# Splitting the weight operands of a Strassen-like matmul two at a time, in double-size tiles

## The chip, the cores and the metric

One core of one Trainium2 chip runs the kernel. Its engines are TensorE (PE: matmuls, and PEld for its weight loads), VectorE (DVE), ScalarE (ACT), GpSimd (POOL) and the queues that start transfers (SP above all). The metric is the device time of one execution in microseconds (us); the lower, the better. Each engine works off its own instructions in a fixed order, and one that waits holds up all behind it on that engine.

## The reference, cut to what matters

One layer of a decoder trunk over x (1024 tokens, 1024 channels) and 256 memory tokens. Nearly all of the work is matrix products with 1024 x 1024 weights:

```
h  = rms_norm(x, norm_g)
z  = h @ w_in                      # 11 blocks of 1024 columns
u  = gelu(z[U]);  v = layer_norm(gelu(z[V]))
br_a = u * (causal 128x128 mix of v inside each chunk, 8 groups, + b_s) * silu(z[GA])
glu  = z[BA] * sigmoid(z[BB])
br_b = silu(layer_norm(depthwise_causal_conv(glu, 31 taps))) * silu(z[GB])
br_c = cross_attention(z[Q], rms_norm(mem), w_kv) * silu(z[GC])
merged = sum over n of sigmoid(z[M0 + n]) * (br_n @ w_branch[n])
y = rms_norm(x + merged @ w_out, final_norm_g)
```

All of it is float32. To keep float32's accuracy on TensorE, an operand is split into a rounded high part and the remainder (hi and lo, both in the type fp32r), and a product is the sum of three: hi by hi, hi by lo, lo by hi.

## The kernel before

**Stages.** The kernel first makes keys and values of the memory and branch v. Then come 40 "pairs": in four rounds p = 0..3, ten blocks of w_in each (i = 0..9: BB, BA, U, GA, GC, GB, Q and three merge-gate blocks), and each pair computes two 128-channel rows of a block for all 1024 tokens. After the pairs come the projections of branches a and c with the attention between them, and then two more large products (branch b's projection and w_out), called the output stages here, and the final norm.

**A pair** (`pair`, L463 to L518) is a 2 x 2 block product with seven instead of eight block products. Its weights are two raw tiles r0 and r1 of 128 x 1024, loaded by SP; their halves are a11, a12 and a21, a22. DVE forms s1 = a21 + a22 (L460), s2 = s1 - a11 (L461), s3 = a11 - a21 (L479) and s4 = a12 - s2 (L480). Each of the seven weight operands a11, a12, s2, s1, s3, a22, s4 (128 x 512) is split by `operand`: ACT casts the high part (L74), DVE subtracts it (L75) to get the low part. `prod` (L448) then issues 12 matmuls of 128 x 512 per operand: for each of four k the high part twice, against the high and the low part of the other matrix, and after these the low part once. The seven products go to three PSUM banks x, z and y: x<-B (with a11) and z<-B (a12), x<-T (s2), y<-T (s1), x<-T (s3), and, put off into the next pair as fin1 and fin2, x<-T (a22) and y<-B (s4). ACT copies x out between (p1 at L466, u2 at L489, u3 at L498); DVE adds the halves of the result together in the tiles ca and cb (L476, L501, L511). In the trace the raw operands' tiles read `op<-raw`, the sums' `op<-sum`.

**What sets the order.** Tiles come from rings: `op` has 6 tiles of 128 x 2 x 512, `sum` 4 and `half` 4 of 128 x 512, `raw` 3 of 128 x 1024, `slot` 39 of 128 x 1024. A tile that is taken waits until the tile's last user is done. A scheduler orders the instructions of each engine when the program is built; no table in the kernel fixes them, beside a few that are kept in program order. Between the pair's steps, `fill` lets DVE do a few of the conv branch's 120 tap steps per round (L553: one multiply-add over 128 x 994 to 1023). The pair with the block GA ends with `ugate` (L624 to L636): DVE multiplies by u (L624), 32 small matmuls on PE mix v (L630), and DVE scales (L632) and multiplies four times (L636). Its instructions stand in the pair after the next on DVE, that is at i = 5. Each round also prepares sums of weight blocks in `wsums`: loads on SP, adding transfers on POOL, a split of 128 x 1024 (`wsh<-ws` on ACT, `ws<-ws,wsh` on DVE), and two stores to DRAM that POOL issues through L149 (`sw<-wsh` and `sw<-ws`). The tile `wsh` is of the `slot` ring, as ca and cb are.

**The output stages** take their operands through `gop` (a tile of the `op` ring each) and `gop2` (a `sum` and a `half` tile) in turn, and `oprod` (L979) issues their matmuls.

Of the kernel before, what the change touches and what calls it, by code (L numbers as in the profile page):

```python
# [16 lines left out]
P = 128  # L17
# [4 lines left out]
H = 512  # L22
# [17 lines left out]
def trunk(ctx, tc, xt, x, memt, wf, wv, wkf, wkv, mem, wbr, wb1, wo, wst, bs, cols, fng, out):  # L40
# [13 lines left out]
    def nm(s):  # L54
        uid[0] += 1
        return f"{s}_{uid[0]}"

    def slot(dt=F32, shape=(P, 1024), s="s"):
        return slots.tile(list(shape), dt, tag="slot", name=nm(s))

    def op(shape=(P, 2, H), s="op"):
        return wpool.tile(list(shape), F32R, tag="op", name=nm(s), bufs=NOP)

    def half(s="u"):
        return wpool.tile([P, H], F32, tag="half", name=nm(s), bufs=NHALF)

    def bank(s="b"):
        return bank1.tile([P, H], F32, tag="b", name=nm(s))
# [4 lines left out]
    def split(src, hi, lo):  # L73
        A.copy(hi, src)  # L74
        V.tensor_tensor(lo, src, f(hi), ALU.subtract)  # L75
# [9 lines left out]
        return raw  # L85

    def wchunk(src, raw=None):
        hi, lo = op((P, 1024), "whi"), op((P, 1024), "wlo")
        split(raw_load(src) if raw is None else raw, hi, lo)
        return hi, lo  # L90

    def flat(ps):
        return ps.rearrange("p a b -> p (a b)")
# [165 lines left out]
    for g in range(2):  # L259
        pst = [bank() for _ in range(4)]  # L260
        for j in range(4):
            i = 4 * g + j
            if i == 0:
                hi, lo = op((P, 1024), "whi"), op((P, 1024), "wlo")
                for kk2 in range(2):
                    v = slice(kk2 * H, (kk2 + 1) * H)
                    ksplit(kraw[0][:, v], hi[:, v], lo[:, v])
                    mem_gain(kk2)
            elif g:
                hi, lo = wchunk(None, kraw[i])  # L270
            else:
                hi, lo = op((P, 1024), "whi"), op((P, 1024), "wlo")
                ksplit(kraw[i], hi, lo)
                if g == 0:
                    mem_gain(2 * j)
                    mem_gain(2 * j + 1)
            for kk2 in range(2):
                k = 2 * j + kk2
                for e in range(4):
                    ks = slice(kk2 * H + e * P, kk2 * H + (e + 1) * P)  # L280
                    for n, (w, m) in enumerate(((hi, mhi), (hi, mlo), (lo, mhi))):
                        T.matmul(pst[e][:, :M], w[:, ks], m[k], start=(k == 0 and n == 0),
                                 stop=(k == KT - 1 and n == 2))
            kload(i + 3)
            if i < MT:
                sload(mtok[i], mem[i * P:(i + 1) * P, :])
            elif i < 5:
                x_load(2 * i - 4)
                x_load(2 * i - 3)
            else:  # L290
                v_load(i - 5)
                x_load(i + 1)
            if i == 3:
                for t in range(MT):
                    square(mtok[t], mss[:, t:t + 1])
                mr = mean_rsqrt(mss, MT, RMS_EPS)
                mdg = diagonals(mr, MT)
            if i == 5:
                spread(mdg, mrb, bank)
            if i >= 4:  # L300
                x_gain(i - 4)
            if i >= 6:
                for _ in range(2):
                    k_out(*late.pop(0))
        if g == 0:
            k3 = half("k3")
            A.copy(k3[:, :M], pst[3][:, :M])
            pst[3] = k3
        late.extend((4 * g + e, pst[e]) for e in range(4))
# [134 lines left out]
    def prod(ps, w, m, start, stop):  # L444
        for k in range(4):
            ks = slice(k * P, (k + 1) * P)
            for j, (a, b) in enumerate(((0, 0), (0, 1), (1, 0))):
                T.matmul(ps, w[:, a, ks], m[k][:, b, :], start=(start and k == 0 and j == 0),  # L448
                         stop=(stop and k == 3 and j == 2), skip_group_check=not start)

    def operand(src):
        o = op()
        split(src, o[:, 0, :], o[:, 1, :])
        return o

    def pair(blk, p, consume, fill=lambda: None, last=False):
        r0, r1 = raw_load(wf[blk, 2 * p]), raw_load(wf[blk, 2 * p + 1])
        a11, a12, a21, a22 = r0[:, :H], r0[:, H:], r1[:, :H], r1[:, H:]
        s1, s2, s3, s4 = [wpool.tile([P, H], F32, tag="sum", name=nm("sum"), bufs=NSUM) for _ in range(4)]
        V.tensor_tensor(s1, a21, a22, ALU.add)  # L460
        V.tensor_tensor(s2, s1, a11, ALU.subtract)  # L461
        o11 = operand(a11)
        x, z = bank("x"), bank("z")  # L463
        prod(x, o11, B[0][0], True, True)
        p1 = half("p1")
        A.copy(p1, x)  # L466
        fill()
        if pend:
            pend.pop(0)()
        fill()  # L470
        ca, cb = slot(s="ca"), slot(s="cb")

        def second():
            o12 = operand(a12)
            prod(z, o12, B[1][0], True, True)
            V.tensor_tensor(ca[:, :H], z, p1, ALU.add)  # L476
            fill()

        V.tensor_tensor(s3, a11, a21, ALU.subtract)  # L479
        V.tensor_tensor(s4, a12, s2, ALU.subtract)  # L480
        if not last:
            second()
        if pend:
            pend.pop(0)()
        fill()
        os2 = operand(s2)
        prod(x, os2, T2, False, True)
        u2 = half("u2")
        A.copy(u2, x)  # L489
        fill()  # L490
        os1 = operand(s1)
        y = bank("y")
        prod(y, os1, T1, True, True)
        fill()
        os3 = operand(s3)
        prod(x, os3, T3, False, True)
        u3 = half("u3")
        A.copy(u3, x)  # L498
        if last:
            second()  # L500
        V.tensor_tensor(cb[:, H:], y, u3, ALU.add)  # L501
        fill()
        o22 = operand(a22)
        os4 = operand(s4)

        def fin1():
            prod(x, o22, T4, False, True)

        def fin2():
            prod(y, os4, B[1][1], False, True)  # L510
            V.tensor_tensor(ca[:, H:], y, u2, ALU.add)  # L511
            consume(ca, cb, x)

        pend.extend((fin1, fin2))
# [286 lines left out]
    def att_q(n):  # L801
        hd, tb = divmod(n, 2)
        if hd not in kv:
            kv_load(hd)
        qh, ql = slot(F32R, (P, 2, H), "qh"), slot(F32R, (P, 2, H), "ql")
        for d in range(2):
            qf = wpool.tile([P, H], F32, tag="sum", name=nm("qf"), bufs=NSUM)
            nc.sync.dma_start(out=qf, in_=qdram[2 * hd + d][:, tb * H:(tb + 1) * H])
            split(qf, qh[:, d, :], ql[:, d, :])
        unit[n] = (qh, ql)  # L810
# [132 lines left out]
    def swload(w, i, tag):  # L943
        r = []
        for j in range(2):
            hl = [op((P, 1024), "sw") if tag else slot(F32R, s="sw") for _ in range(2)]
            b = (SUMB, SUMO)[w][i]
            if i == "1" or len(b) > 1:
                for v in range(2):
# [15 lines left out]
            split(v, q[:, 0, :], q[:, 1, :])  # L965
        return q[:, 0, :], q[:, 1, :]

    def top2(v):
        hi = wpool.tile([P, H], F32R, tag="sum", name=nm("bhi"), bufs=NSUM)
        lo = wpool.tile([P, H], F32R, tag="half", name=nm("blo"), bufs=NHALF)  # L970
        split(v, hi, lo)
        return hi, lo

    def oprod(ps, a, w, start):
        for t in range(4):
# [32 lines left out]
    b11, b21 = [[cm[4 * r + k][:, :H] for k in range(4)] for r in range(2)]  # L1008
    b12, b22 = [[cm[4 * r + k][:, H:] for k in range(4)] for r in range(2)]
    sw1 = swload(0, "1", True)  # L1010
    o11 = [top2(v) for v in b11]
    sw2 = swload(0, "2", False)
    pxy = [acc() for _ in range(4)]
    px, py = [[t[:, i, :] for t in pxy] for i in range(2)]
# [14 lines left out]
    oprod(px, sw6, o6, False)  # L1029
    sw5 = swload(0, "5", False)  # L1030
    o5 = [top(v, True) for v in t1]
    u2 = copies(px, lambda: wpool.tile([P, H], F32, tag="sum", name=nm("u2"), bufs=NSUM))
    oprod(py, sw5, o5, True)
    sw7 = swload(0, "7", True)
    for k in range(4):
# [17 lines left out]
    gf = merged  # L1053


    def gop(v):
        o = op()
        split(v, o[:, 0, :], o[:, 1, :])
        return o[:, 0, :], o[:, 1, :]

    def gop2(v):
        hi = wpool.tile([P, H], F32R, tag="sum", name=nm("ahi"), bufs=NSUM)
        lo = wpool.tile([P, H], F32R, tag="half", name=nm("alo"), bufs=NHALF)
        split(v, hi, lo)
        return hi, lo

    def quad(r, c):
        return [gf[4 * r + k][:, c * H:(c + 1) * H] for k in range(4)]
# [56 lines left out]
        (A if i == 3 else nc.sync).dma_start(out=out[rows, w:], in_=v[:, w:])  # L1125

    a11, a12, a21, a22 = quad(0, 0), quad(1, 0), quad(0, 1), quad(1, 1)
    o = [gop(v) for v in a11]
    oprod(px, o, w, True)
    o, w = [gop2(v) for v in a12], wn  # L1130
    wn = swload(1, "6", False)
    yload(0)
    fg = load(fng.broadcast_to([P, D]), s="fg")
# [5 lines left out]
    sums4(s2, s1, a11)  # L1139
    yadd(0, 0, px)  # L1140
    oprod(py, o, w, True)
    o, w = [gop(v) for v in s2], wn
    sums4(a21, a11, a21)
    wn = swload(1, "5", False)
    yadd(0, 0, py, 1)
    oprod(px, o, w, False)
    o, w = [gop2(v) for v in s1], wn
    wn = swload(1, "7", False)
    yadd(0, 1, px, 0, ALU.subtract)
    oprod(py, o, w, True)  # L1150
    o, w = [gop(v) for v in a21], wn
    wn = swload(1, "4", False)
    yload(1)
    yadd(1, 1, py)
    oprod(px, o, w, False)
    o, w = [gop2(v) for v in a22], wn
    wn = swload(1, "3", False)
    yadd(1, 1, px, 1, ALU.subtract)
    oprod(px, o, w, False)
    sums4(a12, a12, s2, ALU.add)  # L1160
    o, w = [gop(v) for v in a12], wn
    yadd(1, 0, px, 2)
    oprod(py, o, w, False)
    yadd(0, 1, py, 2)
# [10 lines left out]
NFETCH = 3  # L1175
NSLOT = 39
NRAW = 3
NOP = 6
NSUM = 4
NHALF = 4  # L1180
PUMPA = 8
NWARM = 10
# [60 lines left out]
```

## Time and profile before

| | us |
|---|---|
| median of three runs (lowest, highest) | 1317.36 (1316.32, 1318.34) |
| the profiled execution's own time | 1315.63 |
| its span | 1313.9 |
| PE busy, of the span | 1301.2 (99%) |
| PEld / DVE busy | 1085.8 (83%) / 1088.4 (83%) |
| ACT / POOL busy | 616.9 (47%) / 115.5 (9%) |

The span runs from the first to the last instruction of the profiled execution. The mean granted clock of TensorE is 0.998 of full speed. A share is an average over all stages; the stage of the pairs takes 142.7 to 920.7 us of the span. Matmuls are pipelined, so each lists more time (390 ns) than lies between two starts.

### The profile page before, as it was taken

What the parts mean: (1) busy time and instruction counts of PE and PEld (TensorE: products, weight loads), DVE (VectorE), ACT (ScalarE), POOL (GpSimd) and SP (SyncE); (2) the same over time, 40 slices, a digit from 0 to 9 for tenths busy, and PEclk for the clock granted to TensorE, in tenths of its full rate; (3) what the DMA queues carried; (4) which work ended last, traced back from release to release, by engine and by line L of the source; (5) the groups of instructions that cost most, each with busy time, mean ns of one, the idle gap of its engine ahead of it and who ended that gap; (6) DMA issues with size and microseconds to landing.
All of it is one profiled execution on the core that took longest, in us unless ns stands there. A gap on an engine that the chain in (4) does not pass through costs nothing.

```text
span 1313.9 us, 16329 instructions
## 1 busy us (share of the span) xinstructions
PE 1301.2 (99%) x6010; PEld 1085.8 (83%) x6010; DVE 1088.4 (83%) x1468; ACT 616.9 (47%) x1012; POOL 115.5 (9%) x194
## 2 busy tenths in 40 slices
PE   9999999999999999999999999999999999999997
PEld 8788888888888888888888888888888888888886
DVE  6889669989959989976998996896589478895886
ACT  7667644445344445444444434445544443443245
POOL 0100000211000212001111101001000010000000
PEclk9999999999999999999999999999999999999999
DMA  9944324787425777325778436447553654655933
GB/s 340 411 158 153 136 81 132 223 270 219 139 82 161 216 225 239 130 80 166 231 232 244 129 94 158 170 172 255 194 198 123 207 194 144 224 193 220 406 126 128
DMA packets 82016, 249.74 MB, mean 190 GB/s; under 512 B 8336, under 2 KB 18064, under 8 KB 81936
## 3 DMA queue, kind: packets, MB, share of 16 engines
q1 hardware_dynamic: 55552, 153.44, 33.4%
q0 software_dynamic: 26096, 94.91, 23.2%
q8 instruction: 47, 0.77, 0.2%
q10 hardware_dynamic: 288, 0.35, 0.1%
q14 instruction: 33, 0.27, 0.1%
HBM read 176.84 MB, written 68.16 MB: 186 GB/s over the span
## 4 chain that ended last, share of the span: by engine, by line
PE 92%; DMA 4%; ACT 1%; DVE 1%; issue 1%; SPq 0%; POOL 0%; ACTq 0%; POOLq 0%
PE x L448 33%; PE y L448 17%; PE acc L778 12%; PE acc L979 10%; PE z L448 8%; PE b L402 7%; PE acc L819 2%; PE acc L855 1%; DMA raw<-in_wv 1%; PE sp L630 1%; DMA kvraw<-in_wkv 1%; DMA k<-kd 1%; PE acc L840 0%; ACT y L1124 0%; DMA mtok<-in_mem 0%
## 5 line engine op out<-in xcount | busy, mean ns | idle before, releaser
L448 PE MATMUL x<-T,op 128*128 128x512 f32 x1440 | 347.4, 390 | 0.0
L448 PEld LDWEIGHTS x<-T,op 128*128 128x128 f32 x1440 | 270.0, 188 | 56.3 <-ACT u L489 0.5
L74 ACT CAST op<-sum 128x512 fp32r<-128x512 f32 x160 | 99.4, 622 | 122.2 <-PE z L448 57.8
L553 DVE SCALAR_TENSOR_TENSOR conv<-cb,col,conv 128x994 f32<-128x994 f32 (+14 forms) x120 | 151.9, 1266 | 1.3 <-ACT conv L549 0.5
L75 DVE TENSOR_TENSOR op<-sum,op 128x512 fp32r<-128x512 f32 x160 | 109.6, 685 | 24.8 <-ACT op L74 24.6
L448 PE MATMUL x<-B,op 128*128 128x512 f32 x480 | 115.5, 389 | 0.0
L448 PE MATMUL z<-B,op 128*128 128x512 f32 x480 | 115.3, 389 | 0.0
L448 PE MATMUL y<-T,op 128*128 128x512 f32 x480 | 115.3, 389 | 0.0
L448 PE MATMUL y<-B,op 128*128 128x512 f32 x480 | 115.3, 389 | 0.0
L553 DVE SCALAR_TENSOR_TENSOR conv<-ca,col,conv 128x994 f32<-128x994 f32 (+14 forms) x90 | 113.7, 1264 | 0.4
L74 ACT CAST op<-raw 128x512 fp32r<-128x512 f32 x120 | 74.3, 620 | 73.2 <-PE y L448 71.8
L448 PEld LDWEIGHTS z<-B,op 128*128 128x128 f32 x480 | 90.1, 188 | 18.7
L448 PEld LDWEIGHTS y<-T,op 128*128 128x128 f32 x480 | 90.1, 188 | 18.7
L448 PEld LDWEIGHTS y<-B,op 128*128 128x128 f32 x480 | 90.1, 188 | 18.7
L448 PEld LDWEIGHTS x<-B,op 128*128 128x128 f32 x480 | 90.1, 188 | 18.7
L75 DVE TENSOR_TENSOR op<-raw,op 128x512 fp32r<-128x512 f32 x120 | 82.2, 686 | 24.4 <-ACT op L74 24.1
L778 PE MATMUL acc<-bhi,whi 128*128 128x512 f32 x256 | 79.7, 393 | 0.9 <-DVE ca L511 0.9
L778 PE MATMUL acc<-bhi,wlo 128*128 128x512 f32 x256 | 79.2, 390 | 0.0
L778 PE MATMUL acc<-blo,whi 128*128 128x512 f32 x256 | 79.2, 390 | 0.0
L979 PE MATMUL acc<-q,sw 128*128 128x512 f32 x288 | 65.4, 389 | 0.0
L979 PEld LDWEIGHTS acc<-q,sw 128*128 128x128 f32 x288 | 54.1, 188 | 11.2
L498 ACT COPY u<-x 128x512 f32<-128x512 f32 x40 | 23.6, 589 | 81.6 <-PE x L448 81.6
(267 smaller groups left out, 2162.1 us busy)
## 6 DMA issues: line engine op xcount, KB each, us to landing
raw<-in_wf SPq DMA_DIRECT2D x80, 512.0 KB, 3.6
sw<-sw SPq DMA_DIRECT2D x40, 512.0 KB, 7.8
sw<-wsh POOLq DMA_DIRECT2D x20, 512.0 KB, 4.3
sw<-ws POOLq DMA_DIRECT2D x20, 512.0 KB, 3.9
raw<-in_wv SPq DMA_DIRECT2D x16, 512.0 KB, 4.0
raw<-in_wbr SPq DMA_DIRECT2D x16, 512.0 KB, 5.5
gate<-g SPq DMA_DIRECT2D x16, 512.0 KB, 4.4
ws<-in_wb POOLq DMA_DIRECT2D x14, 512.0 KB, 6.4
```

The costliest lines, as they stand in the source:

```text
L74: A.copy(hi, src)
L75: V.tensor_tensor(lo, src, f(hi), ALU.subtract)
L402: T.matmul(pst[t], q[:, a, ts_], w[:, ws], start=(k == 0 and j == 0), stop=(k == KT - 1 and j == 2))
L448: T.matmul(ps, w[:, a, ks], m[k][:, b, :], start=(start and k == 0 and j == 0), stop=(stop and k == 3 and j == 2), skip_group_check=not start)
L498: A.copy(u3, x)
L553: V.scalar_tensor_tensor(out=a[:, PAD - j:], in0=g[:, :n], scalar=col[:, cw + j:cw + j + 1], in1=a[:, PAD - j:], op0=ALU.mult, op1=ALU.add)
L630: T.matmul(ps[:, t * P:(t + 1) * P], va[:, 4 * hf + t, :], ws[:, i, :], start=True, stop=True)
L778: T.matmul(ps[:, hf, :], w[:, ks], m[k][:, hf * H:(hf + 1) * H], start=(k == 0 and j == 0), stop=(k == KT - 1 and j == 2))
L819: T.matmul(ps[:, i, :], q[a][:, d, i * P:(i + 1) * P], kk[:, b, d, :], start=(d == 0 and j == 0), stop=(d == 1 and j == 2))
L855: T.matmul(ps[:, d, :], vv[:, a, m, d * P:(d + 1) * P], p2[b][:, m, :], start=(m == 0 and j == 0), stop=(m == MT - 1 and j == 2))
L979: T.matmul(ps[t], a[k][i][:, ts_], w[k][n], start=(start and k == 0 and j == 0), stop=(k == 3 and j == 2), skip_group_check=not start)
```

## The change

The seven operands of a pair are split in four steps instead of seven. `operands` takes a whole 128 x 1024 tile: r0 gives a11 and a12 in one cast and one subtraction, the tile s2 | s1 gives os2 and os1, and s4 | a22 gives os4 and o22, for which s4 is written over a21 in r1. Only s3 is still split alone, into a tile of the `sum` ring instead of the `op` ring, with s3 itself in a `half` tile. The `op` ring has 3 tiles of twice the size instead of 6, the `sum` ring 2 of twice the size instead of 4. In `second`, o12's split no longer stands ahead of z's product. Everywhere else the same rings are taken in double tiles: `wchunk`, `ksplit`'s callers and `swload` put hi and lo of one weight tile into one `op` tile, and `gop` and `gop2` become `gops` and `tops`, which take their tiles two at a time but split one operand at a time as before. Line numbers grow by 9 to 11 there: L75 is L84, L448 is L459, L460 is L472, L461 is L473, L476 is L487, L479 is L490, L480 is L491, L501 is L512, L511 is L521, L553 is L563, L624, L632 and L636 are L634, L642 and L646.

```diff
+    def wide(dt=F32, s="sum"):
+        return wpool.tile([P, 2 * H], dt, tag="sum", name=nm(s), bufs=NSUM)
+
+    def halves(t):
+        return t[:, :H], t[:, H:]
...
-    def operand(src):
+    def operands(src):
         o = op()
         split(src, o[:, 0, :], o[:, 1, :])
-        return o
+        return [(o[:, 0, v], o[:, 1, v]) for v in (slice(0, H), slice(H, 2 * H))]
...
-        s1, s2, s3, s4 = [wpool.tile([P, H], F32, tag="sum", name=nm("sum"), bufs=NSUM) for _ in range(4)]
+        s12, s3 = wide(), half("s3")
+        s2, s1 = halves(s12)
         V.tensor_tensor(s1, a21, a22, ALU.add)
         V.tensor_tensor(s2, s1, a11, ALU.subtract)
-        o11 = operand(a11)
+        o11, o12 = operands(r0)
...
         def second():
-            o12 = operand(a12)
             prod(z, o12, B[1][0], True, True)
...
-        V.tensor_tensor(s4, a12, s2, ALU.subtract)
+        V.tensor_tensor(a21, a12, s2, ALU.subtract)
...
-        os2 = operand(s2)
+        os2, os1 = operands(s12)
...
-        os1 = operand(s1)
...
-        os3 = operand(s3)
+        os3 = halves(wide(F32R, "os3"))
+        split(s3, *os3)
...
-        o22 = operand(a22)
-        os4 = operand(s4)
+        os4, o22 = operands(r1)
...
+    def tops(vs):
+        r = []
+        for v, hi in zip(vs, wides(4, F32R, "bhi")):
+            lo = half("blo", F32R)
+            split(v, hi, lo)
+            r.append((hi, lo))
+        return r
...
+    def gops(vs):
+        r = []
+        for v0, v1 in (vs[:2], vs[2:]):
+            o = op()
+            for v, q in ((v0, slice(0, H)), (v1, slice(H, 2 * H))):
+                split(v, o[:, 0, q], o[:, 1, q])
+                r.append((o[:, 0, q], o[:, 1, q]))
+        return r
...
-NOP = 6
-NSUM = 4
+NOP = 3
+NSUM = 2
```

**DVE in an ordinary pair.** In round 1, where no conv step stands between them, the order of before (number at a name's end: one tile of it; `op_3326` is a11's low part, `op_3362` a12's, `op_3396` s2's) is:

```order
L479 TENSOR_TENSOR sum_3322<-raw_3316,raw_3318 128x512
L75 TENSOR_TENSOR op_3305<-raw_3175,op_3305 128x512
L476 TENSOR_TENSOR ca_3215<-z_3187,p_643_3200 128x512
L75 TENSOR_TENSOR op_3308<-sum_3180,op_3308 128x512
L480 TENSOR_TENSOR sum_3323<-raw_3316,sum_3321 128x512
L511 TENSOR_TENSOR ca_3073<-y_3134,u_627_3128 128x512
L75 TENSOR_TENSOR op_3326<-raw_3316,op_3326 128x512
L75 TENSOR_TENSOR op_3362<-raw_3316,op_3362 128x512
L75 TENSOR_TENSOR op_3396<-sum_3321,op_3396 128x512
L460 TENSOR_TENSOR sum_3467<-raw_3465 128x512
L501 TENSOR_TENSOR cb_3216<-y_3272,u_652_3301 128x512
```

and now (`op_3160` is the tile of a11 and a12, `op_3227` of s2 and s1, `op_3144` of s4 and a22 of the pair before, `os_560` that of s3):

```order
L490 TENSOR_TENSOR s_550_3025<-raw_3020,raw_3022 128x512
L491 TENSOR_TENSOR raw_3022<-raw_3020,sum_3024 128x512
L84 TENSOR_TENSOR os_560_3125<-s_550_3025,os_560_3125 128x512
L472 TENSOR_TENSOR sum_3156<-raw_3154 128x512
L487 TENSOR_TENSOR ca_3060<-z_3032,p_554_3045 128x512
L473 TENSOR_TENSOR sum_3156<-sum_3156,raw_3152 128x512
L84 TENSOR_TENSOR op_3144<-raw_3022,op_3144 128x1024
L521 TENSOR_TENSOR ca_2929<-y_2984,u_542_2981 128x512
L84 TENSOR_TENSOR op_3160<-raw_3152,op_3160 128x1024
L84 TENSOR_TENSOR op_3227<-sum_3156,op_3227 128x1024
L512 TENSOR_TENSOR cb_3061<-y_3111,u_561_3140 128x512
```

Low parts of 128 x 512 have become low parts of 128 x 1024, and s2's sum (L473) stands ahead of the tile of a11 and a12.

**DVE at the gate in round 2.** The pair is i = 5 (block GB), and the gated block's `ca_5006`, `cb_5007` are being finished. Before, a11's low part (`op_5311`) stands ahead of the gate's instructions:

```order
L511 TENSOR_TENSOR ca_5006<-y_5068,u_926_5062 128x512
L75 TENSOR_TENSOR op_5311<-raw_5301,op_5311 128x512
L632 SCALAR_TENSOR_TENSOR sp_5198<-sp_5198,col,bsb_4820 128x512
L476 TENSOR_TENSOR ca_5160<-z_5132,p_946_5145 128x512
L624 TENSOR_TENSOR ca_5006<-ca_5006,ca_4866 128x1024
L632 SCALAR_TENSOR_TENSOR sp_5205<-sp_5205,col,bsb_4820 128x512
L636 TENSOR_TENSOR ca_5006<-ca_5006,sp_5198 128x512
```

and a12's (`op_5348`) behind the last of them:

```order
L636 TENSOR_TENSOR cb_5007<-cb_5007,sp_5220 128x512
L553 SCALAR_TENSOR_TENSOR conv_5249<-ca_4723,col,conv_5249 128x994
L75 TENSOR_TENSOR op_5348<-raw_5301,op_5348 128x512
L553 SCALAR_TENSOR_TENSOR conv_5249<-ca_4723,col,conv_5249 128x995
L75 TENSOR_TENSOR op_5384<-sum_5306,op_5384 128x512
```

Now, ahead of the gate's instructions on the same engine:

```order
L84 TENSOR_TENSOR op_4983<-raw_4824,op_4983 128x1024
L472 TENSOR_TENSOR sum_4998<-raw_4996 128x512
L521 TENSOR_TENSOR ca_4719<-y_4775,u_776_4772 128x512
L642 SCALAR_TENSOR_TENSOR sp_4897<-sp_4897,col,bsb_4546 128x512
L487 TENSOR_TENSOR ca_4862<-z_4834,p_792_4847 128x512
```

and at their end, where `op_5002` is the tile of a11 and a12:

```order
L646 TENSOR_TENSOR cb_4720<-cb_4720,sp_4912 128x512
L646 TENSOR_TENSOR cb_4720<-cb_4720,sp_4919 128x512
L563 SCALAR_TENSOR_TENSOR conv_4948<-ca_4458,col,conv_4948 128x994
L473 TENSOR_TENSOR sum_4998<-sum_4998,raw_4994 128x512
L563 SCALAR_TENSOR_TENSOR conv_4948<-ca_4458,col,conv_4948 128x995
L84 TENSOR_TENSOR op_5002<-raw_4994,op_5002 128x1024
L512 TENSOR_TENSOR cb_4863<-y_4950,u_804_4979 128x512
```

The low part of a11 has moved from ahead of the gate's first instruction to behind its last one and two conv steps, and s2's sum with it. The same holds in round 1 and 3; in round 0 a11's low part stood behind the gate's instructions before, too.

**PE at that place.** Before, the product of a11 (`x_5314`, 12 matmuls) was followed by others:

```order
L448 MATMUL x_5314<-B_1102,op_5311 128x512 x3
L448 MATMUL x_5314<-B_1188,op_5311 128x512 x3
L448 MATMUL x_5314<-B_1282,op_5311 128x512 x3
L448 MATMUL x_5314<-B_1368,op_5311 128x512 x3
L448 MATMUL x_5131<-T_1154,op_5287 128x512 x3
L448 MATMUL x_5131<-T_1240,op_5287 128x512 x3
L448 MATMUL x_5131<-T_1334,op_5287 128x512 x3
L448 MATMUL x_5131<-T_1420,op_5287 128x512 x3
L448 MATMUL z_5315<-B_1106,op_5348 128x512 x3
```

and now:

```order
L459 MATMUL x_5005<-B_1077,op_5002 128x512 x2
L459 MATMUL z_5006<-B_1081,op_5002 128x512 x2
L459 MATMUL x_5005<-B_1077,op_5002 128x512
L459 MATMUL x_5005<-B_1161,op_5002 128x512 x3
L459 MATMUL x_5005<-B_1253,op_5002 128x512 x3
L459 MATMUL x_5005<-B_1337,op_5002 128x512 x3
L459 MATMUL x_4833<-T_1128,op_4983 128x512 x3
L459 MATMUL x_4833<-T_1212,op_4983 128x512 x3
L459 MATMUL x_4833<-T_1304,op_4983 128x512 x3
L459 MATMUL x_4833<-T_1388,op_4983 128x512 x3
L459 MATMUL z_5006<-B_1081,op_5002 128x512
L459 MATMUL z_5006<-B_1165,op_5002 128x512 x3
```

Two matmuls of z's product, both with the high part of a12, now stand between the first two of x's, both with the high part of a11, and the rest of x's. In round 0 one of z's stands there. Elsewhere the order of PE's products is as it was.

## Rows read from the trace of the kernel before

**Rows 1.** Engines over the span: busy us, share, instructions

```profile
PE 1301.2 (99%) x6010; PEld 1085.8 (83%) x6010; DVE 1088.4 (83%) x1468; ACT 616.9 (47%) x1012; POOL 115.5 (9%) x194
```

**Rows 2.** Waits of PE: line waited for, us in total, times, longest

```profile
PE warm L206 <- POOL ones L161: 1.1, 1, 1.1
...
PE b L350 <- DVE wlo L75: 0.3, 1, 0.3
```

**Rows 3.** Groups of splits by form: busy us, mean ns, idle before

```profile
L75 DVE TENSOR_TENSOR op<-sum,op 128x512 fp32r<-128x512 f32 x160 | 109.6, 685 | 24.8 <-ACT op L74 24.6
L74 ACT CAST op<-sum 128x512 fp32r<-128x512 f32 x160 | 99.4, 622 | 122.2 <-PE z L448 57.8 <-PE y L448 43.1 <-issue 13.3
...
L75 DVE TENSOR_TENSOR wlo<-raw,whi 128x1024 fp32r<-128x1024 f32 x32 | 38.9, 1219 | 14.0 <-ACT whi L74 9.8 <-PE y L448 4.1
L74 ACT CAST whi<-raw 128x1024 fp32r<-128x1024 f32 x32 | 33.6, 1054 | 48.1 <-PE acc L778 30.8 <-DMA raw<-in_wv 7.0 <-PE b L402 3.6
```

**Rows 4.** Timeline of one pair in round 1: start us, us, engine, line, operation

```profile
362.03 2.88 PE L448 MATMUL x<-T,op 128*128 128x512 f32 x12
362.23 0.62 ACT L74 CAST op<-raw 128x512 fp32r<-128x512 f32 x1 [2.04 <-PE y L448]
...
362.89 0.69 DVE L75 TENSOR_TENSOR op<-raw,op 128x512 fp32r<-128x512 f32 x1
...
370.19 2.88 PE L448 MATMUL x<-B,op 128*128 128x512 f32 x12
```

**Rows 5.** Window 205 to 340: PE, PEld, DVE, ACT, POOL busy, PEclk, DMA

```profile
205.00:340.00 135.00, 135.00 (x613) 112.40 (x612) 130.06 (x163) 62.59 (x97) 20.72 (x34) 1.00 0.67 211
```

**Rows 6.** Timeline around the gate in round 2 (in brackets: idle before, releaser)

```profile
612.09 0.56 POOL L149 DMA_DIRECT2D sw<-wsh  x1 [1.87 <-ACT wsh L74]
...
614.93 0.69 DVE L75 TENSOR_TENSOR op<-raw,op 128x512 fp32r<-128x512 f32 x1
...
618.60 0.69 DVE L476 TENSOR_TENSOR ca<-z,p 128x512 f32<-128x512 f32 x1 [2.30 <-DMA sw<-wsh]
...
624.70 1.25 DVE L553 SCALAR_TENSOR_TENSOR conv<-ca,col,conv 128x994 f32<-128x994 f32 x1
...
625.83 2.88 PE L448 MATMUL x<-B,op 128*128 128x512 f32 x12
625.87 0.68 DVE L75 TENSOR_TENSOR op<-raw,op 128x512 fp32r<-128x512 f32 x1
```

**Rows 7.** SP's queue in the same stretch

```profile
611.33 15.58 SPq L82 DMA_DIRECT2D raw<-in_wf  x2
```

**Rows 8.** Transfers by line: KB each, median us from issue to landing

```profile
sw<-wsh POOLq DMA_DIRECT2D x20, 512.0 KB, 4.3
```

**Rows 9.** Timeline around the gate in round 0

```profile
229.24 1.22 DVE L75 TENSOR_TENSOR ws<-ws,wsh 128x1024 fp32r<-128x1024 f32 x1
230.37 0.68 DVE L476 TENSOR_TENSOR ca<-z,p 128x512 f32<-128x512 f32 x1
...
234.68 0.69 DVE L75 TENSOR_TENSOR op<-raw,op 128x512 fp32r<-128x512 f32 x1
235.28 0.69 DVE L480 TENSOR_TENSOR sum<-raw,sum 128x512 f32<-128x512 f32 x1
...
236.91 2.88 PE L448 MATMUL x<-B,op 128*128 128x512 f32 x12
```

**Rows 10.** Timeline around the gate in round 3

```profile
818.15 1.27 DVE L636 TENSOR_TENSOR cb<-cb,sp 128x512 f32<-128x512 f32 x2
819.35 0.68 DVE L75 TENSOR_TENSOR op<-raw,op 128x512 fp32r<-128x512 f32 x1
...
820.29 2.88 PE L448 MATMUL x<-B,op 128*128 128x512 f32 x12
```

**Rows 11.** Timeline of round 2, pair i = 6, and the output stage's tightest operand

```profile
643.54 0.68 DVE L75 TENSOR_TENSOR op<-raw,op 128x512 fp32r<-128x512 f32 x1
...
644.87 2.88 PE L448 MATMUL x<-B,op 128*128 128x512 f32 x12
...
1229.52 4.70 PE L979 MATMUL acc<-sw,op 128*128 128x512 f32 x20
...
1230.32 0.69 DVE L75 TENSOR_TENSOR op<-gate,op 128x512 fp32r<-128x512 f32 x1
```

## What is predicted, and from what

> **What bounds the kernel now.** I read the page's table of engines first. PE is busy for 1301.2 of a span of 1313.9 us, while DVE stands at 83% and ACT at 47% [rows 1]. Since the busy time of pipelined matmuls can hide gaps, the waits of PE come next: there are seven rows, from 1.1 us down to 0.3 us, 4.2 us in all, and the two shown stand for their kind: start-up, the memory's keys, one hand-over [rows 2]. None of them is in a pair. The timeline gives PE's pace: from the product of s2 at 362.03 to the next pair's first product at 370.19 there are three products, 8.16 us, so 2.72 us for one of 12 matmuls, 0.227 us for a matmul, 19.04 us for a pair of seven [rows 4]. The granted clock there is full, and PE is busy in every microsecond [rows 5]. What a change to ACT and DVE can do is then read from one number only: how long before its product an operand's low part is ready.
>
> That number is comfortable in an ordinary pair. The low part of a11 ends at 362.89 + 0.69 = 363.58 us, and its product starts at 370.19: 6.6 us to spare [rows 4]. It is small where DVE is full. In 205 to 340 us DVE is busy 130.06 of 135 us, 96% [rows 5], and at the gate in round 0 the low part starts at 234.68 for a product at 236.91, 1.5 us to spare [rows 9]. In round 2 at i = 6 it ends at 644.22 for a product at 644.87, 0.65 us [rows 11].
>
> **The change, part by part.**
>
> *Fewer, longer splits.* A cast of 128 x 512 takes 622 ns, one of 128 x 1024 takes 1054; the subtraction 685 and 1219 [rows 3]. In each pair six of each become three: ACT 6 x 0.622 - 3 x 1.054 = 0.57 us less, DVE 6 x 0.685 - 3 x 1.219 = 0.45 us less. Over 40 pairs that is 23 us of ACT and 18 us of DVE. Durations overlap a little, so for DVE I take starts: a 128 x 512 one holds the engine 0.60 us (234.68 to 235.28), a 128 x 1024 one 1.13 (229.24 to 230.37) [rows 9]; 6 x 0.60 - 3 x 1.13 = 0.2 us per pair, 8 us in all. All of it lies beside PE's 19.04 us per pair, so it is worth nothing on the path. Waits that it could shorten are at most PE's 4.2 us, of which none is for a pair's operand: I take 0.
>
> *A later first operand.* a11 must now wait for a12: its cast lasts 0.43 us longer, its subtraction 0.53. With 6.6 us to spare this leaves 5.6 in an ordinary pair: 0. Where the margin was 0.65 us, at i = 6 of round 2, it would be late by 0.3 if nothing else moved; but the product there needs the low part only after two matmuls with the high part, 0.45 us later, so 0 again, as long as DVE is no later than before.
>
> *The low part moved behind the gate.* This is where I see a price. In round 2 it stood ahead of the gate's block, at 614.93; the product came at 625.83 [rows 6]. In the changed order it stands behind the block, one conv step, s2's sum and a second conv step. The block's end is given by the trace: the first conv step starts at 624.70 and the next instruction at 625.87, so a conv step holds DVE 1.17 us [rows 6]. Then 624.70 + 1.17 + 0.60 + 1.17 = 627.64 is the start of the wide subtraction, 628.86 its end. PE can do four matmuls first (two of x, two of z, all with high parts), 625.83 + 0.91 = 626.74. The stall is 2.1 us. That is the upper bound if the gate's block starts when it did. It started late for a reason: the instruction at its head waited 2.30 us for the store `sw<-wsh`, whose tile it takes over [rows 6]. The store was issued at 612.09 and was over at about 618.5, 6.4 us, while such stores take 4.3 in the median [rows 8]; a raw load had gone out just ahead of it at 611.33 [rows 7], and in the changed kernel that load waits for the wide split of s4 and a22, some microseconds later. If the store lands in 4.3 us, at 616.4, all but 0.2 of the wait goes and the stall with it. So the bounds are 0 and 2.1; I take 1.2, a little above the middle, since the wait itself is unchanged and DVE has 0.6 us for s1 inserted ahead.
>
> *The same in the other rounds.* In round 3 the block's last multiplications are followed at 819.35 by the next instruction; now s2's sum and the wide subtraction come there, 819.35 + 0.60 + 1.22 = 821.17, and the product at 820.29 needs it after two matmuls, at 820.74: 0.4 us late [rows 10]. Its block, too, was held by such a store, so 0 to 0.4: I take 0.2. In round 0 the low part was behind the block already; it now has s1 (0.60) and its own longer run (0.53) ahead of its end: 234.68 + 0.69 + 1.13 = 236.5, and the product needs it at 236.91 + 3 x 0.227 = 237.6 [rows 9]: 0, at most 0.3. In round 1 the gate's block did not wait for a store and ends earlier against its product: 0.
>
> *Rings.* The bytes are the same. A double tile comes free only when its later half does; but each of the three takes over the tile of the same kind one pair before, whose products are done by then, so nothing is added. In the output stage the tightest operand ends at 1231.01, and the ninth matmul after 1229.52, at 1231.56, needs it [rows 11]: 0.55 us. With pairs of tiles the second one can wait for one matmul more, 0.23 us. Between 0 and 0.3 (if the subtraction behind it slips a place), I take 0.1.
>
> **The sum.** 0 + 1.2 + 0.2 + 0.1 = 1.5 us longer, between 0 and 3.1. Against the profiled execution's own 1315.63 us that is 1317.1; that execution lay 1.73 us under the median of 1317.36, so the median of the changed kernel comes to 1318.9.
>
> **What the Trainium skill says against it.** The row first: nothing in a pair waits for ACT or DVE on PE [rows 2], and DVE has 17% of the span free [rows 1]. "Perfetto Trace Analysis", Optimizing Scalar/DVE Operations, says that grouping pays on a saturated engine, and that where one is not saturated but causes bubbles elsewhere, smaller instructions may let work finish sooner. By that rule the change does harm exactly where an operand is the last thing waited for, which is the gate in round 2; without the rule the sum is the same.
>
> **Rivals.**
>
> (a) *DVE becomes the bound behind the gate: slower.* Place: pairs i = 5 to 9 of round 2 and the filled stretch of round 0. DVE's work there is 96% of 19.04 us, 18.3 us per pair [rows 5], 0.7 us under PE. The scheduler places conv steps by its own idea of DVE's speed; if the new order sets one more conv step (1.17 us) ahead of a wide subtraction, its pair is late by up to 1.17 - 0.7 = 0.5 us, again and again. It decides from the point where the low part of a11 comes later than 0.45 us after its product's place. Price: 2.1 + 0.4 + 0.3 for the gates, 0.3 in the output stage and 0.5 x 5 to 7 pairs, 5.6 to 6.6 us: 1323 to 1324. For it: margins of 0.65 and 1.5 us. Against: each pair gives DVE 0.2 us back, and the margins grow again from pair to pair.
>
> (b) *PE has headroom that DVE or ACT withholds: faster.* For it: weight loads are busy only 83% [rows 1]. Against: the pace of 2.72 us holds where operands are ready 6.6 us ahead [rows 4]. What could be won is PE's waits, 4.2 us, at most with the span's 12.7 us without PE: 1313.2 if all the waits went. "Perfetto Trace Analysis", Identifying the Most-Contended Engine, judges PE by the weight loads' busy share rather than by the matmuls'; by it 17% would be open. The even spacing of the starts speaks against that here.
>
> (c) *Nothing reaches PE.* The store lands early, the gate's block starts earlier and all stalls vanish: 1317.4. The store's 4.3 us in the median [rows 8] speaks for it, and the raw load that is only put off and may still meet it, against.
>
> **Chances.** My forecast, a stall of 0.5 to 2.5 us in sum: 0.45, 1317.9 to 1319.9. (c): 0.27. Between forecast and (a), sums of 2.5 to 5 us, from both gates in full and some late pairs: 0.13. (a): 0.10. (b) or some gain that I do not see: 0.05. A measurement of this kernel can tell about 0.2%, 2.63 us, from no change: faster is under 1314.7, slower over 1320.0. Of (a) and the case beside it nearly all is slower, of the forecast its top edge, in sum 0.22; of (b) nearly all is faster, 0.04; the rest, 0.74, is the same. The range: from 1316.0, since (c) with the runs' own spread of 1 us reaches there, to 1321.6, which holds the full price of the gates (3.1) and one or two late pairs (1.1).
>
> **What would show it.** In the trace of the changed kernel the groups of subtractions should read 128x1024 in 120 instances near 1.22 us and casts near 1.05, with DVE's busy share some 1% lower and PE's still 99%. The waits of PE should have a new row, x L459 waiting for DVE op L84, of 0.5 to 2.2 us as its longest, at about 626 us, and a smaller one at 820. No such row, with L487 at the gate starting near 616.5, is (c). Such a row with many instances between 626 and 720 or 205 and 340 is (a). A pair of less than 19.04 us would be (b) and prove the reading of PE's pace wrong. The forecast is wrong if the waits come for a transfer or for ACT, or lie outside the gates.

## The result, and the profile after

The changed kernel took 1336.34 us in the median of four runs (1334.55 to 1339.21), against 1316.84 for the kernel before: 1.0151 times as long, 95% interval 1.0127 to 1.0174. The forecast was 1318.9 in a range of 1316.0 to 1321.6. It was wrong: slower by 19.5 us instead of 1.5.

The profiled execution took 1335.50 us with a span of 1333.5, 19.6 more than before. The engines of the kernel after, to be held against [rows 1]:

```profile
PE 1307.3 (98%) x6010; PEld 1089.3 (82%) x6010; DVE 1079.4 (81%) x1348; ACT 606.1 (45%) x892; POOL 114.2 (9%) x194
```

DVE and ACT do less, as worked out: DVE is busy 9 us less, ACT 11. The groups of subtractions of the kernel after (busy us, mean ns, idle before) answer to [rows 3]:

```profile
L84 DVE TENSOR_TENSOR op<-raw,op 128x1024 fp32r<-128x1024 f32 x80 | 97.6, 1221 | 1.6 <-ACT op L83 1.5
L84 DVE TENSOR_TENSOR op<-sum,op 128x1024 fp32r<-128x1024 f32 x40 | 48.8, 1221 | 24.1 <-ACT op L83 24.0
L84 DVE TENSOR_TENSOR os<-s,os 128x512 fp32r<-128x512 f32 x40 | 27.5, 688 | 10.0 <-ACT os L83 10.0
```

The waits of PE (line waited for, us in total, times, longest) name the loss at once. Their first row is new against [rows 2]:

```profile
PE x L459 <- ACT u L500: 13.7, 5, 4.2
PE warm L215 <- POOL ones L170: 1.1, 1, 1.1
```

It is the product of s3, which waits five times until ACT has copied u2 out of the bank x. The first of the five, in the timeline of the kernel after (pair 8, counted from 0 through all rounds; in brackets the idle time before and what ended it):

```profile
300.47 0.69 DVE L490 TENSOR_TENSOR s<-raw,raw 128x512 f32<-128x512 f32 x1
...
302.25 0.69 DVE L491 TENSOR_TENSOR raw<-raw,sum 128x512 f32<-128x512 f32 x1
...
303.00 5.10 SPq L91 DMA_DIRECT2D raw<-in_wf  x2
...
304.99 2.88 PE L459 MATMUL x<-T,op 128*128 128x512 f32 x12
...
307.71 2.88 PE L459 MATMUL y<-T,op 128*128 128x512 f32 x12
...
311.18 0.69 DVE L472 TENSOR_TENSOR sum<-raw 128x512 f32<-128x512 f32 x1 [3.44 <-DMA raw<-in_wf]
311.79 0.68 DVE L521 TENSOR_TENSOR ca<-y,u 128x512 f32<-128x512 f32 x1
...
312.51 1.06 ACT L528 ACTIVATE ca<-ca 128x1024 f32<-128x1024 f32 x1 [6.27 <-DVE ca L521]
...
313.47 0.57 ACT L500 COPY u<-x 128x512 f32<-128x512 f32 x1
...
314.09 4.60 PE L459 MATMUL x<-T,os 128*128 128x512 f32 x12 [3.50 <-ACT u L500]
```

Read it from the end. PE waits for the copy u2. On ACT the copy stands behind the activation of the pair before, and this waits for the addition L521. On DVE the addition stands behind s1 of the *next* pair (L472), and s1 waits for its raw tile r1. The load of r1 goes out at 303.00, when s4 (L491) of this pair has read the last of r0, whose tile it takes, and it takes 8.2 us to release s1. The same pair before, where that load goes out at 290.88, s1 of the next pair begins 9 us ahead of the addition and the copy comes in time:

```profile
282.08 0.69 DVE L479 TENSOR_TENSOR sum<-raw,raw 128x512 f32<-128x512 f32 x1
...
290.88 0.33 SPq L82 DMA_DIRECT2D raw<-in_wf  x1
...
296.20 0.68 DVE L460 TENSOR_TENSOR sum<-raw 128x512 f32<-128x512 f32 x1
...
305.11 0.69 DVE L511 TENSOR_TENSOR ca<-y,u 128x512 f32<-128x512 f32 x1
...
307.83 0.59 ACT L489 COPY u<-x 128x512 f32<-128x512 f32 x1 [0.93 <-PE x L448]
```

L479 is s3. Before, it ran at 282.08, 12 us ahead of its pair's first product (294.03); after, at 300.47, 6.4 us behind it (294.11). Over pairs 2 to 38 the median went from 12.5 us ahead to 4.2 behind, and that of s4 from 6.7 ahead to 6.0 behind. The waits of DVE for r1 (before, after) doubled:

```profile
DVE sum L460 <- DMA raw<-in_wf: 23.5, 13, 4.9
```

```profile
DVE sum L472 <- DMA raw<-in_wf: 48.6, 20, 5.0
```

What the loads themselves wait for changed with it. In SP's queue the largest row of before is for low parts, the largest of after for s4, 40 times for 40 pairs:

```profile
SPq L82 <- DVE op L75: 678.9, 77, 14.8
```

```profile
SPq L91 <- DVE raw L491: 511.3, 40, 17.6
```

**The account.** The gaps between starts of PE's matmuls at the five waits are 3.89, 2.27, 1.31, 4.58 and 3.55 us, 0.23 of each the usual: 14.5 us lost. After each of the three long ones (the first, the fourth and the fifth) the product that had waited is slow itself. The windows of the kernel after around the first wait (us, then busy time of PE, PEld, DVE, ACT, POOL, the granted clock, DMA share, GB/s):

```profile
300.00:310.40 10.40, 10.40 (x47) 8.45 (x45) 7.70 (x9) 3.22 (x4) 1.99 (x3) 1.00 0.80 224
310.50:314.00 3.50, 0.09 (x1) 0.00 (x0) 2.82 (x4) 1.49 (x3) 0.00 (x0) 1.00 0.57 227
314.10:318.50 4.40, 4.40 (x12) 3.52 (x13) 4.33 (x5) 0.88 (x1) 0.53 (x1) 0.61 0.29 119
318.60:330.00 11.40, 11.40 (x52) 9.45 (x51) 11.37 (x13) 5.21 (x8) 2.52 (x4) 1.00 0.54 143
```

PE does nothing for 3.5 us and then gets a mean clock of 0.61 for 4.4 us; its matmuls start 0.43 us apart for the first eight, half the speed, and the product takes 4.44 us to the next one's start instead of 2.72. The three slow products cost 1.72, 1.72 and 1.47 us, those after the two short waits 0.14 each: 5.2. Together 19.7, and PE's last matmul starts 19.75 us later than before (1325.20 against 1305.45).

### The profile page after: what moved, and what is told of

The parts are those of the page before. It is cut to its first block, busy times and chain, and to the rows that moved or that the text cites. A ratio compares the mean times of both kernels' runs of the same rounds, so it can differ in the third digit from the quotient of the medians.

```text
span 1333.5 us, 16070 instructions
## 1 busy us (share of the span) xinstructions
PE 1307.3 (98%) x6010; PEld 1089.3 (82%) x6010; DVE 1079.4 (81%) x1348; ACT 606.1 (45%) x892; POOL 114.2 (9%) x194
## 4 chain that ended last, share of the span: by engine, by line
PE 77%; DVE 9%; DMA 9%; issue 3%; ACT 2%; SPq 0%; POOL 0%; DVEq 0%; ACTq 0%
PE x L459 25%; PE y L459 12%; PE acc L788 12%; PE acc L996 10%; PE b L413 7%; PE z L459 6%; DMA raw<-in_wf 5%; DVE conv L563 4%; PE acc L830 2%; PE acc L866 1%; DMA raw<-in_wv 1%; DVE op L84 1%; PE sp L640 1%; DMA kvraw<-in_wkv 1%; DMA k<-kd 1%
## 5 line engine op out<-in xcount | busy, mean ns | idle before, releaser
L459 PE MATMUL x<-T,op 128*128 128x512 f32 x960 | 231.9, 390 | 0.0
L459 PEld LDWEIGHTS x<-T,op 128*128 128x128 f32 x960 | 179.9, 188 | 37.2
L563 DVE SCALAR_TENSOR_TENSOR conv<-cb,col,conv 128x994 f32<-128x994 f32 (+14 forms) x120 | 151.7, 1264 | 1.9 <-ACT conv L559 0.5
L788 PE MATMUL acc<-bhi,w 128*128 128x512 f32 x512 | 141.3, 392 | 0.9 <-DVE ca L521 0.9
L83 ACT CAST op<-raw 128x1024 fp32r<-128x1024 f32 x80 | 84.2, 1054 | 120.5 <-PE z L459 58.0
L459 PE MATMUL x<-T,os 128*128 128x512 f32 x480 | 120.6, 402 | 13.7 <-ACT u L500 13.7
L459 PEld LDWEIGHTS x<-T,os 128*128 128x128 f32 x480 | 93.0, 195 | 35.6 <-ACT u L500 16.1
L459 PE MATMUL x<-B,op 128*128 128x512 f32 x480 | 115.8, 389 | 0.0
L459 PE MATMUL z<-B,op 128*128 128x512 f32 x480 | 115.6, 389 | 0.0
L459 PE MATMUL y<-T,op 128*128 128x512 f32 x480 | 115.3, 389 | 0.0
L459 PE MATMUL y<-B,op 128*128 128x512 f32 x480 | 115.3, 389 | 0.0
L563 DVE SCALAR_TENSOR_TENSOR conv<-ca,col,conv 128x994 f32<-128x994 f32 (+14 forms) x90 | 113.7, 1264 | 0.7
L788 PEld LDWEIGHTS acc<-bhi,w 128*128 128x128 f32 x512 | 95.2, 188 | 20.9 <-ACT bhi L83 1.4
L459 PEld LDWEIGHTS x<-B,op 128*128 128x128 f32 x480 | 90.1, 188 | 18.8
L459 PEld LDWEIGHTS y<-B,op 128*128 128x128 f32 x480 | 90.1, 188 | 18.7
L459 PEld LDWEIGHTS z<-B,op 128*128 128x128 f32 x480 | 90.1, 188 | 18.7
L459 PEld LDWEIGHTS y<-T,op 128*128 128x128 f32 x480 | 90.1, 188 | 18.7
L84 DVE TENSOR_TENSOR op<-raw,op 128x1024 fp32r<-128x1024 f32 x80 | 97.6, 1221 | 1.6 <-ACT op L83 1.5
L788 PE MATMUL acc<-blo,w 128*128 128x512 f32 x256 | 79.1, 390 | 0.0
L84 DVE TENSOR_TENSOR op<-sum,op 128x1024 fp32r<-128x1024 f32 x40 | 48.8, 1221 | 24.1 <-ACT op L83 24.0
L472 DVE TENSOR_TENSOR sum<-raw 128x512 f32<-128x512 f32 x40 | 27.5, 688 | 48.7 <-DMA raw<-in_wf 48.6
```

Source lines behind the costliest of these rows:

```text
L459: T.matmul(ps, w[a][:, ks], m[k][:, b, :], start=(start and k == 0 and j == 0), stop=(stop and k == 3 and j == 2), skip_group_check=not start)
L563: V.scalar_tensor_tensor(out=a[:, PAD - j:], in0=g[:, :n], scalar=col[:, cw + j:cw + j + 1], in1=a[:, PAD - j:], op0=ALU.mult, op1=ALU.add)
L788: T.matmul(ps[:, hf, :], w[:, ks], m[k][:, hf * H:(hf + 1) * H], start=(k == 0 and j == 0), stop=(k == KT - 1 and j == 2))
```

## The experiments

Theory A: it is s3's new place, in the `half` ring beside p1, u2 and u3, not the wide splits. Theory B blames the wide splits, theory C other transfers in the queues; the expectation of e2 spells all three out. Tiles of a ring seem to be handed out in program order, so s3 can't be formed before u3 of the pair before has its tile. On DVE, s3 ran ahead of the pair before's addition into cb (which reads u3) in all 39 pairs that have one before them in the kernel before, and in none of them in the changed kernel. All kernels are timed against runs of the kernel before beside them (median 1315.9 to 1316.2 us).

**e1: the control.** `NSLOT = 39` becomes 38, to make room.

> The changed kernel with 38 slot tiles in place of 39, to make room in the next two; nothing else. Both theories: no difference from the changed kernel, 1333 to 1340 us, with the same kind of waits of PE (x<-T of s3 waiting for the copy u2 on ACT, 10 to 18 us in all).

1338.89 us (ratio 1.0171, 1.0155 to 1.0187); five waits for u2, 9.8 us, just under the 10 expected, and one of 3.4 us near 238 that the changed kernel with 39 slots doesn't have. One slot less moves the waits about. The median is 2.6 us above the changed kernel's, but the runs of the two overlap, so a cost of the slot itself isn't shown.

**e2: s3 in a ring of its own.**

```diff
-NSLOT = 39
+NSLOT = 38
-        s12, s3 = wide(), half("s3")
+        s12, s3 = wide(), wpool.tile([P, H], F32, tag="s3", name=nm("s3"), bufs=1)
```

> As the control with 38 slots, but s3 gets a ring of its own (one tile of 128 x 512) in place of a tile of the ring that p1, u2 and u3 share. The wide splits stay. Theory A (s3 shares that ring, whose tiles are handed out in program order, so s3 is formed only after u3 of the pair before; that holds r0, hence the load of the next r1, hence s1 of the next pair, behind which on DVE stands the addition that ACT and then PE wait for): the stalls go, 1316 to 1320 us, and s3 stands some 10 us earlier against its pair. Theory B (the wide splits themselves hold DVE and ACT too long at a time, and u2's copy is late for that): no change, 1333 to 1340 us. Theory C (the loads are late because of other transfers in the queues, whatever the order): stalls remain, 1325 to 1340 us.

1322.95 us (1.0048, 1.0035 to 1.0061): between A and the rest, outside A's numbers by 3 us. All waits for u2 are gone, DVE waits 7.6 us for r1. But the waits of PE have a new first row:

```profile
PE x L459 <- DVE op L84: 4.0, 2, 2.0
```

They are waits of the very kind that the prediction had: the product of a11 for the wide low part, at 236.9 (the gate of round 0) and 647.4 us (i = 6 of round 2). Timeline of the latter:

```profile
647.19 0.61 PE L459 MATMUL x<-B,op 128*128 128x512 f32 x2
647.88 0.68 DVE L473 TENSOR_TENSOR sum<-sum,raw 128x512 f32<-128x512 f32 x1
648.49 1.22 DVE L84 TENSOR_TENSOR op<-raw,op 128x1024 fp32r<-128x1024 f32 x1
...
649.62 1.25 DVE L563 SCALAR_TENSOR_TENSOR conv<-ca,col,conv 128x1004 f32<-128x1004 f32 x1
...
649.76 3.36 PE L459 MATMUL x<-B,op 128*128 128x512 f32 x10 [1.96 <-DVE op L84]
```

Two matmuls with the high part go, the ten others wait until the subtraction that began at 648.49 is done.

**e3: four raw tiles, s3 left where it is.** `NSLOT = 38`, `NRAW = 3` becomes 4.

> As the control with 38 slots, but four raw tiles in place of three, s3 left in the shared ring. Theory A: the load of the next r1 no longer waits for s3 and s4, s1 waits for it at most now and then, 1317 to 1323 us, though s3 stays as late against its pair as in the changed kernel. Theory B: no change, 1333 to 1340 us. Theory C: some of the waits go, 1322 to 1336 us.

1316.69 us (1.0003, 0.9994 to 1.0012): the time of the kernel before, and no wait for u2. s3 still runs behind cb's addition in 38 of the 39 pairs, but r1 no longer waits for r0's tile; the waits of DVE:

```profile
DVE sum L472 <- DMA raw<-in_wf: 1.5, 1, 1.5
```

So the late s3 costs through the load, anything else being at most the 0.12% of the interval, and A's middle link holds. C falls too: the kernel moves the same 249.7 MB, and the waits are gone.

**e4: the kernel before with s3 in the shared ring, and nothing else.**

```diff
-        s1, s2, s3, s4 = [wpool.tile([P, H], F32, tag="sum", name=nm("sum"), bufs=NSUM) for _ in range(4)]
+        s1, s2, s4 = [wpool.tile([P, H], F32, tag="sum", name=nm("sum"), bufs=NSUM) for _ in range(3)]
+        s3 = half("s3")
```

> The kernel before with one thing of the change alone: s3 taken from the ring that p1, u2 and u3 share. All splits stay single, s4 has its own tile. Theory A: s3 goes behind u3 of the pair before, r0 is held as in the changed kernel, and the stalls appear: 1322 to 1338 us, PE waiting for u2's copy. Theory B: no wide splits, so no stalls: 1315 to 1319 us. Theory C: as B, 1315 to 1319 us.

1324.35 us (1.0066, 1.0054 to 1.0079), with all splits single. The waits of PE, and the same chain in its timeline (lines are one higher than before here):

```profile
PE x L448 <- ACT u L490: 4.0, 3, 1.9
```

```profile
307.06 0.69 DVE L461 TENSOR_TENSOR sum<-raw 128x512 f32<-128x512 f32 x1 [2.47 <-DMA raw<-in_wf]
...
308.85 0.68 DVE L512 TENSOR_TENSOR ca<-y,u 128x512 f32<-128x512 f32 x1
...
309.56 1.06 ACT L519 ACTIVATE ca<-ca 128x1024 f32<-128x1024 f32 x1 [5.04 <-DVE ca L512]
...
310.53 0.57 ACT L490 COPY u<-x 128x512 f32<-128x512 f32 x1
...
311.15 1.21 PE L448 MATMUL x<-T,op 128*128 128x512 f32 x4 [1.84 <-ACT u L490]
```

B fails: no wide split, and the same wait. Only a conv step stands between s1 and the addition here. The loads now wait for s3 (L480):

```profile
SPq L82 <- DVE s L480: 525.9, 38, 19.1
```

It is 8.4 us and not 19.5. A likely reason is that s4 has its own tile here and runs ahead of s3, so that r0 comes free with s3 (in the median 3.9 us behind its pair's first product) and not with s4 (6.0 us behind it in the changed kernel). How much of the difference that makes wasn't taken apart: the 11 us between the two are not shown to come from it.

**e5: a fifth tile in the shared ring** (`NHALF = 5`, `NSLOT = 38`).

> As the control with 38 slots, but the ring of p1, s3, u2 and u3 has five tiles in place of four. Theory A (the ring's program order delays s3, and u2's copy waits on ACT behind the activation of the pair before): a fifth tile changes neither; s3 stays behind the addition into cb of the pair before in every pair, 1333 to 1342 us, five or so waits for u2's copy. Theory D (the ring is simply too small: u2's copy waits for a tile that is still read): the stalls go, 1316 to 1325 us.

1339.20 us (1.0178, 1.0164 to 1.0192), five waits for u2, 9.9 us: as the control. The number of tiles is not it; sharing is. Theory D is out.

**e6: the changed kernel's bytes and 39 slots, s3 in one tile of its own.**

```diff
-        s12, s3 = wide(), half("s3")
+        s12, s3 = wide(), wpool.tile([P, H], F32, tag="s3", name=nm("s3"), bufs=1)
-NHALF = 4
+NHALF = 3
```

> The changed kernel with all 39 slots and the same bytes: s3 gets one tile of its own, and the ring of p1, u2 and u3 has three tiles in place of four. Theory A: no wait for u2's copy of over 1 us is left; what remains are waits for the low part of a11 and a12, none to two of 2 us as in the run with 38 slots: 1316 to 1323 us. Theory D: with three tiles the waits for u2's copy are as many or more, 1333 us and over.

1317.29 us (1.0008, 1.0000 to 1.0017). s3 is ahead again in all 39 pairs, and no wait in a pair is left; the longest waits of PE:

```profile
PE b L413 <- ACT w L83: 1.2, 1, 1.2
PE warm L215 <- POOL ones L170: 1.1, 1, 1.1
PE acc L788 <- DVE ca L521: 0.9, 1, 0.9
```

The loads wait for s4 8 times instead of 40:

```profile
SPq L91 <- DVE raw L491: 42.6, 8, 7.3
```

With the wide splits in full the kernel is at the time of before, to within 0.2%.

**e7: e2 with a11 and a12 split one after the other.**

```diff
-        o11, o12 = operands(r0)
+        od = op()
+        o11, o12 = [(od[:, 0, v], od[:, 1, v]) for v in (slice(0, H), slice(H, 2 * H))]
+        split(a11, *o11)
...
         def second():
+            split(a12, *o12)
```

> 38 slots, s3 in a ring of its own, and a11 and a12 split one after the other again (into halves of one double tile); the other two double splits stay. If the two waits of 2 us that were left with s3's own ring (x<-B for the low part, at the gate of round 0 and at i = 6 of round 2) come from the wide first operand, they go: 1315.5 to 1318.5 us. If they come from the other wide splits or from DVE's load, they stay: 1320 to 1324 us.

1319.27 us (1.0027, 1.0017 to 1.0037). The two waits shrink from 4.0 to 1.7 us but stay: the wide first operand is more than half of them. What the rest is wasn't tested; in e2 DVE was busy for all of 640 to 650 us, at the second of them. Neither expectation was met whole.

**e8: the kernel before with four raw tiles** (`NRAW = 4`, `NSLOT = 38`).

> The kernel before with 38 slots and four raw tiles. Theory A: the kernel before waits for nothing that a fourth raw tile gives, 1315 to 1318 us, so that the run of the changed kernel with four raw tiles shows a cost removed. Otherwise a fourth tile is a gain of its own: under 1313 us.

1317.25 us (1.0011, 1.0002 to 1.0020): no gain. What e3 won back was a cost of the change.

**e9: the changed kernel with s1 and the addition into ca kept in program order.**

```diff
-        V.tensor_tensor(s1, a21, a22, ALU.add)
+        keep(V.tensor_tensor(s1, a21, a22, ALU.add))
...
-            V.tensor_tensor(ca[:, H:], y, u2, ALU.add)
+            keep(V.tensor_tensor(ca[:, H:], y, u2, ALU.add))
```

> The changed kernel with its rings as they are, 39 slots; only the sum s1 and the addition of y and u2 into ca are kept in program order on DVE, so that s1 of the next pair stands behind that addition in all but 8 of the pairs (before it stood ahead in 24). s3 and the load of r1 stay as late. Of the five pairs whose wait was seen (s1 of pairs 9, 11, 12, 21 and 29 counted from 0 was the one that waited), 9, 11 and 29 are turned round, 12 and 21 are not. Theory A, the link over DVE's order: the waits of PE near 310, 354 and 714 us go, those near 375 and 552 may stay, 1318 to 1330 us. Rival: u2's copy is late for the load itself or for another instruction, whatever stands first on DVE: five or so waits, 1332 to 1341 us.

1356.73 us (1.0309, 1.0292 to 1.0326), which no theory had. The waits of PE (the three largest of a pair):

```profile
PE x L459 <- ACT op L83: 15.2, 6, 4.6
PE x L459 <- DVE op L84: 7.5, 3, 4.0
...
PE x L459 <- ACT u L500: 1.1, 1, 1.1
```

Of the five waits for u2 one is left, at 567 us, in a pair that was not turned round (21). Of the two that were allowed to stay, the one near 375 went as well. In pair 8 the next r1 is loaded from 317.51 on and takes 6.7 us, to 324.2; the addition L521 runs at 322.01, ahead of its landing, the copy u2 follows at 323.91, and the product of s3 starts at 326.37 without a wait. So far the link over DVE's order holds. But s1 behind the addition is late for its own operand: PE now waits for the wide split of s2 and s1. The order that the scheduler had chosen was the better one, given a late r1.

## Why the prediction was wrong, by its own steps

**PE as the bound, no gain.** Right. DVE's 8 us less by starts were measured as 9, ACT's group sums fell from 173.7 to 151.3 us, 22 less for 23, and nothing of it shortened a product. PE's pace stayed 2.72 us, so rival (b) falls; e6 has the same work with every operand in time and is not faster.

**The rings.** This is the step that failed: "so nothing is added". It looked at what became of the double tiles only. That s3 moved from the `sum` ring to the `half` ring, where it comes behind u3, stands in the diff and in the part on the change; I gave it no term. It is worth 8.4 us alone (e4), and without it the whole change costs 0 to 0.2% (e6; 0.4 to 0.6% with 38 slots, e2). The rest of the 19.5 us comes only where s3's place and the other parts of the change meet, and how isn't shown. With this step fell the premise that everything can be read "from one number only", how early a low part is ready: no low part was late. The wait was for the copy u2, by way of a load.

**The sum s1 ahead of the addition.** The order showed L472 ahead of the gate's instructions and I charged it 0.60 us, its run. Its wait had to be looked at: it was released by a load, up to 4.9 us late already in the row of before, which was not among the rows that the prediction rests on. Behind it on DVE stood an addition for which ACT and then PE wait. That order is not new. Of 38 pairs, s1 of the next pair ran ahead of the addition in 35 before and in 24 after. New is how close the two came: in the median s1 began 8.6 us ahead of the addition before and 0.6 after, so a late load now holds the addition up.

**The low part behind the gate.** The place and the working were right, the stall was not there. The kernel after at round 2's gate, to be held against [rows 6]:

```profile
630.89 0.68 DVE L487 TENSOR_TENSOR ca<-z,p 128x512 f32<-128x512 f32 x1
...
636.99 1.24 DVE L563 SCALAR_TENSOR_TENSOR conv<-ca,col,conv 128x994 f32<-128x994 f32 x1
...
639.92 1.22 DVE L84 TENSOR_TENSOR op<-raw,op 128x1024 fp32r<-128x1024 f32 x1
...
640.77 0.62 PE L459 MATMUL x<-B,op 128*128 128x512 f32 x2
...
641.23 0.62 PE L459 MATMUL z<-B,op 128*128 128x512 f32 x2
...
641.68 2.43 PE L459 MATMUL x<-B,op 128*128 128x512 f32 x10
```

From the first conv step to the wide subtraction it is 2.93 us, 2.94 by the forecast; the ten matmuls follow without a gap. The block's head no longer waits for the store: no idle time stands at L487, where it was 2.30 us. The store was issued 13.7 us ahead of the product in both kernels, so it is the store that landed sooner, and not the product that came later. That was rival (c) at this one place, and the term of 1.2 us was 0. The 0.2 of round 3 and the 0.1 of the output stages were 0 as well: no such wait is in the list of PE's. In e2 such stalls did come, 4.0 us in two: at the gate of round 0, priced at 0 to 0.3, and at i = 6 of round 2, priced at 0. The mechanism is real, and where it strikes hangs on an order that already a slot and a `half` tile more or less change (e2 against e6).

**The slower rival (a).** Slower, but not by its mechanism: nothing was late behind the gate, and at the first wait DVE itself stood idle for 3.44 us. That the forecast had "slower" right is luck as well, since none of its 1.5 us came about. Its own signs of being wrong did: the waits came for ACT, behind it for a transfer, and outside the gates. The Trainium skill's "Perfetto Trace Analysis", Optimizing Scalar/DVE Operations, which would break up instructions where an engine isn't saturated but causes bubbles elsewhere, fits e2 and e7 with 2.3 us (4.0 less 1.7) and nothing in the change itself. Of the 2.3 us, 1.5 came at i = 6 of round 2, where DVE was saturated (busy for all of 640 to 650 us in e2), so that condition didn't hold there.

## What to carry to other kernels

When a tile is moved to another ring, list what shares that ring and when each sharer is taken: a temporary that could be formed early was held here until the ring's earlier sharers had come, with four tiles and with five alike. Then follow what the late temporary keeps alive (here a raw tile, so a load) and what stands behind the load's first reader on its engine. For an instruction that stands ahead of others on its engine, charge its wait, not its run alone.

## What the runs showed of the hardware

A wait of PE can cost more than its length. After the three long waits of the changed kernel (3.3 to 4.4 us without a matmul) the mean granted clock was 0.61, 0.61 and 0.67 over the next 4.4 us, and the product took 1.5 to 1.7 us more, 40 to 47% of the wait on top of it. After the two of 1.1 and 2.0 us it was 1.00, and the product took 0.14 more. The length alone doesn't decide. In e4 two waits of 1.84 and 1.91 us came out differently (windows that begin where the wait ends, columns as above):

```profile
311.10:315.50 4.40, 4.35 (x19) 3.58 (x20) 4.40 (x6) 2.24 (x5) 0.53 (x1) 1.00 0.29 119
722.50:726.90 4.40, 4.32 (x12) 3.41 (x13) 4.40 (x6) 1.07 (x3) 1.43 (x2) 0.61 0.61 98
```

The product after the second took 1.73 us more. What made the difference isn't shown. The slow matmuls started 0.43 us apart, the level of 1.2 GHz, the others 0.23, the level of 2.4 GHz. The Trainium skill, "TensorE: Matmul & The Clock Gate", section "Wait — 56ns, not 53.3ns?", gives 426.7 ns from start to start for 512 columns at the lower level; the trace agrees.
